# Block order and operand addresses of the token mixers, order of the first gates, the second norm and the joint w2 steps in a decoder trunk

## The chip, the core and the metric

The kernel runs on one core of a Trainium2 chip. The metric is the device time of one execution, in microseconds (us). The core's engines work side by side: TensorE (PE in the profile: matmuls, and PEld for the load of the stationary operand), VectorE (DVE), ScalarE (ACT), GpSimd (POOL) and SyncE (SP, which issues DMAs here). Each runs its own instructions in a fixed order and waits on semaphores of the others. Data moves between HBM and the on-chip memory by DMAs, issued from SP (mostly weights) and POOL (mostly spills and their reloads).

## The reference

One block of a decoder trunk on 512 tokens and 16 meta tokens, width 2048, in float32:

```python
u = rmsnorm(h, norm1_g[l])
proj = u @ w_in[l]
v_pool, v_lru, v_gelu, g_pool, g_lru = jnp.split(proj, IN_SPLITS, axis=-1)
pool_out = pool_mixer(v_pool, pool_w[l], pool_scale[l])
xc = causal_depthwise_conv(v_lru, conv_w[l], conv_b[l])
lru_out = rg_lru(xc, ...) * jax.nn.gelu(v_gelu)
merged = jax.nn.sigmoid(g_pool) * pool_out + jax.nn.sigmoid(g_lru) * lru_out
h = h + merged @ w_out[l]
u2 = rmsnorm(h, norm2_g[l])
h = h + jnp.square(jax.nn.relu(u2 @ mlp_w1[l])) @ mlp_w2[l]
out = rmsnorm(h, final_g)
```

`pool_mixer` subtracts each token from its mean over 2, 4, 8 or 16 positions (one width per 512 channels) and multiplies each group by a 512x512 matrix. `rg_lru` has two sigmoid gates per head of 256 channels (8 heads) and a linear recurrence over the positions. Of `w_in` the five parts of 2048 columns are called VP, VL, GE, GP and GL below (pool input, recurrence input, GELU input, two gates).

## The kernel before

Every float32 matrix product is made of three matmuls on a reduced float32 type (fp32r): each operand is the sum of a high and a low part, and `mm3` issues hi x hi, hi x lo and lo x hi into one accumulator. Weights come in tiles of 128x1024 from HBM (tile `raw` or `w`, SP). ACT copies the high part (`whi`, L137), DVE subtracts it for the low one (`wlo`, L138). A class `Weights` keeps the list of loads and splits: `W.next()` hands out the next split weight, `W.advance()` and `W.ready(n)` split ahead, `W.hold` and `W.behind` can tie a split or a sum behind another instruction.

**Mixers (0 to 477 us).** A table of jobs sets their order (the string `jobs`): V2 and VR project two output tiles each while the first norm is still made, VL_c and VP_c one tile of 128 channels each (16 input tiles, each 3 matmuls, over 528 tokens in blocks of 272 and 256 columns), GA_h the recurrence's gates of head h, PW_g the pool matrix of group g, F_k forms operands of the later gate projections and spills them (`fsp`). The activations lie in one tile `a1`; `ux(k, part)` gives the two blocks of input tile k. `products` runs over the two blocks of tokens, inside them over the input tiles that it is given; `in_proj` gives it one input tile at a time for VL and two at a time for VP. A VL tile is evacuated by DVE (`v`, L479) and goes through the convolution; a VP tile by DVE (`pv`, L558), then POOL adds the shifted copies (`pw`, L564), DVE makes the difference (`pd`, L567), and both parts of it go to `dsp_at(c)`, from where PW reads. The last job, PW_3, evacuates its tiles 12 to 15 by ACT (`po`, L586) into four buffers and stores them by DMA (`pl<-po`). The last head's recurrence (`lru`: ACT exp, tanh and Sqrt, DVE products and a scan) runs at the same time.

**Strassen steps.** The gate projections (GL, GE, GP for c = 0 to 7, 477 to 944 us) and the MLP's first matrix (32 steps, 1119 to 1734 us) take seven products of 2x2 blocks instead of eight, in the order x11, t1, t2, x21, t3, x22, t4, on three accumulators A, B and C. t1, t2, t3 and x22's weights are sums or differences, made on DVE (`sum`, `w`, L128). Between the products accumulators are copied by ACT: A after x11 (`p1`), B after t1 (`q5`), A after t2 (`u2`); `put` makes the four output blocks "11", "22", "12", "21". In the very first step (`gl0`) p1 and u2 lie in the tile `scale`. One of the seven input tiles of the gates' operands, k = 7 of x22, is shifted by some columns in its tile.

**Output projection and second norm.** From 945 to 1119 us w_out is multiplied and added to x. Then `middle()` in the first MLP step lets PE sum the squares over the partitions (`ps_r`, L993), from which `rho` follows in five steps on ACT and DVE.

**The second MLP matrix (1734 to 2348 us).** Again Strassen steps, with output tiles of 512 tokens x 256 channels. A few steps are joint (`strassen_pair`, groups [1,3], [2,4] and three at the end): two outputs share one weight, so that everything is done for two accumulators. Of p1, u2 and q5 there the second copy lies in a spare place: p1 and u2 in `scale`, q5 in the last quarter of the second output's tile `e`. The finished tile `e` is added into HBM by an accumulating DMA from POOL (`hsp<-e`, L1115, 512 KB), for groups up to step 31.

The order on each engine comes from a scheduler that keeps the program's order per engine where buffers and dependencies allow; buffers come from pools with a fixed number, and `issue_after` or a manual dependency ties single instructions.

## Time and profile before

| | us |
|---|---|
| median of the runs | 2389.03 (2384.92 to 2390.3, three runs) |
| profiled execution | 2389.73 |
| its span, first to last instruction | 2388.0 |
| first matmul starts | 6.3 |
| DVE busy, ACT busy | 1922.5, 1212.3 |
| mean granted TensorE clock | 0.994 |

A row of the page's list of groups has the line, engine, operation, tiles, shapes and count, then busy time, mean ns of one, and the idle time before it. A row of the waits has the engine and its instruction, the one that released it, and total, times and longest. A row of a timeline has start, duration, engine, line, operation, tiles, shapes and count (neighbours of one kind are merged), and in brackets the idle time before it with what ended it. A row of windows has the stretch, its length, and busy time and count of each engine, then the granted clock, the share of the DMA engines' time and GB/s. Matmuls overlap in their pipeline, so that their pace is read from counts and starts, not from the duration of one.

### The profile page before, as it was taken

The page shows a single profiled execution, that of the slowest core. Times are in us where ns is not written, and L with a number is a line of the kernel's source. Part 1 is how long each engine was busy: PE and PEld are TensorE (multiplying, and loading weights), DVE is VectorE, ACT ScalarE, POOL GpSimd, SP SyncE. Part 2 cuts the span into 40 slices and gives each one's busy share as a digit, 9 for nine tenths or more (in the row PEclk, how much of TensorE's full clock was granted, in tenths as well). Part 3 has the DMA queues.
Part 4 walks back from the last instruction along what each step waited for, and adds up shares of the span by engine and source line. Part 5 has one row for each costly group of instructions (what it writes and reads, how often), then busy time and mean ns, then how long its engine had stood idle before and what let it go on. Part 6 is the DMA issues. An engine that isn't in the chain of part 4 may idle for free. (4 is left out here: it accounts for less than half of the span.)

```text
span 2388.0 us, 46263 instructions
## 1 busy us (share of the span) xinstructions
PE 2347.3 (98%) x19254; PEld 2300.1 (96%) x19254; DVE 1922.5 (81%) x2356; ACT 1212.3 (51%) x1632; POOL 315.5 (13%) x435
## 2 busy tenths in 40 slices
PE   8999999999999999999999999999989999999997
PEld 8999999989999999888999999999989999999997
DVE  7866766588888887378989888888879888888877
ACT  6654645355555554244445444444455555555544
POOL 0224342300000001033000000000110000000013
PEclk9999999999999999999999999999999999999999
DMA  5255554654444447568544544555576666666662
GB/s 198 89 168 173 172 177 166 257 186 150 143 149 143 151 149 261 181 209 283 186 156 153 161 153 159 167 166 162 173 213 173 186 181 182 196 188 188 175 185 107
DMA packets 115858, 418.73 MB, mean 175 GB/s; under 512 B 14112, under 2 KB 18080, under 8 KB 113984
## 3 DMA queue, kind: packets, MB, share of 16 engines
q1 hardware_dynamic: 77040, 253.40, 32.9%
q0 software_dynamic: 38464, 162.29, 21.0%
q8 instruction: 150, 2.46, 0.4%
q14 instruction: 60, 0.49, 0.1%
q10 hardware_dynamic: 144, 0.10, 0.0%
HBM read 324.89 MB, written 90.31 MB: 174 GB/s over the span
## 5 line engine op out<-in xcount | busy, mean ns | idle before, releaser
L138 DVE TENSOR_TENSOR wlo<-raw,whi 128x1024 fp32r<-128x1024 f32 (+2 forms) x388 | 467.2, 1206 | 116.9 <-ACT whi L137 112.9
L137 ACT ACTIVATE whi<-raw 128x1024 fp32r<-128x1024 f32 (+2 forms) x388 | 398.9, 1034 | 318.0 <-issue 78.9
L137 ACT ACTIVATE whi<-sum 128x1024 fp32r<-128x1024 f32 (+3 forms) x267 | 279.0, 1045 | 454.2 <-DVE sum L128 234.8
L138 DVE TENSOR_TENSOR wlo<-sum,whi 128x1024 fp32r<-128x1024 f32 (+3 forms) x267 | 320.1, 1199 | 73.0 <-ACT whi L137 68.1
L370 PE MATMUL ps_A<-a,whi 128*128 128x256 f32 x2048 | 354.5, 277 | 0.0
L370 PE MATMUL ps_Ab<-a,whi 128*128 128x256 f32 x1728 | 308.8, 279 | 4.1 <-ACT u_b L746 2.1
L370 PEld LDWEIGHTS ps_A<-a,whi 128*128 128x128 f32 x2048 | 308.6, 188 | 0.7 <-issue 0.5
L370 PE MATMUL ps_A<-a,wlo 128*128 128x256 f32 x1024 | 282.9, 276 | 0.0
L370 PEld LDWEIGHTS ps_Ab<-a,whi 128*128 128x128 f32 x1728 | 263.9, 190 | 4.7 <-DVE a L1045 2.4
L370 PE MATMUL ps_Ab<-a,wlo 128*128 128x256 f32 x864 | 240.6, 279 | 0.0
L128 DVE TENSOR_TENSOR sum<-sum,raw 128x1024 f32<-128x1024 f32 (+4 forms) x178 | 213.7, 1201 | 5.5
L370 PEld LDWEIGHTS ps_A<-a,wlo 128*128 128x128 f32 x1024 | 192.3, 188 | 0.0
L370 PE MATMUL ps_B<-a,whi 128*128 128x256 f32 x1024 | 177.5, 276 | 0.0
L370 PEld LDWEIGHTS ps_Ab<-a,wlo 128*128 128x128 f32 x864 | 164.2, 190 | 0.0
L370 PE MATMUL ps_vl<-a,whi 128*128 128x272 f32 (+1 forms) x896 | 163.3, 285 | 0.0
L370 PE MATMUL ps_vp<-a,whi 128*128 128x256 f32 (+1 forms) x896 | 162.8, 284 | 0.0
L370 PE MATMUL ps_wo<-a,whi 128*128 128x512 f32 x512 | 158.0, 390 | 0.0
L370 PEld LDWEIGHTS ps_B<-a,whi 128*128 128x128 f32 x1024 | 154.2, 188 | 0.0
L370 PE MATMUL ps_Bb<-a,whi 128*128 128x256 f32 x864 | 152.5, 276 | 0.4 <-DVE a L1045 0.4
L370 PE MATMUL ps_B<-a,wlo 128*128 128x256 f32 x512 | 141.5, 276 | 0.0
L128 DVE TENSOR_TENSOR sum<-w,raw 128x1024 f32<-128x1024 f32 (+3 forms) x89 | 106.5, 1197 | 40.1 <-DMA raw<-w 39.7
L370 PEld LDWEIGHTS ps_vl<-a,whi 128*128 128x128 f32 x896 | 138.2, 189 | 0.3
(336 smaller groups left out, 5854.2 us busy)
## 6 DMA issues: line engine op xcount, KB each, us to landing
raw<-w SPq DMA_DIRECT2D x168, 512.0 KB, 4.3
raw<-w_in SPq DMA_DIRECT2D x135, 512.0 KB, 3.8
w<-w SPq DMA_DIRECT2D x56, 512.0 KB, 4.2
a<-ysp POOLq DMA_DIRECT2D x20, 896.0 KB, 6.1
hsp<-e POOLq DMA_DIRECT2D x33, 512.0 KB, 6.5
ysp<-t POOLq DMA_DIRECT2D x31, 512.0 KB, 4.9
w<-w_in SPq DMA_DIRECT2D x24, 512.0 KB, 3.9
ysp<-y POOLq DMA_DIRECT2D x31, 384.0 KB, 5.1
```

What stands on the lines that cost most here:

```text
L128: nc.vector.tensor_tensor(self.raw[o], self.raw[x], self.raw[y], op=ALU.add)
L137: nc.scalar.activation(hi[:, s], raw[:, s], AF.Copy)
L138: nc.vector.tensor_tensor(lo[:, s], raw[:, s], hi[:, s].bitcast(F32), op=ALU.subtract)
L370: PE.matmul(o, a, b, start=first and i == 0, stop=last and i == 2, skip_group_check=True)
```

## The change

It has five parts. (1) In the mixers `ux` gives other offsets: the blocks of 272 columns lie at 0 (input tiles 0 to 7) or 128 (8 to 15) modulo 256 bytes, those of 256 columns stay at 192, and k % 8 = 7 is shifted by 8 columns (32 bytes) from the others. VL and VP go through half of the input tiles for one block of tokens (8 x 3 = 24 matmuls), then for the other, with tile 7 first. The pool operands move from 192 to 0. (2) In the table of jobs F_3 stands behind VL_8 and PW_1, and the shifted sums of VP_15 are made by DVE. (3) The first gates: po14 and po15 go to a buffer of the pool of sums, both roots stand behind the p1 copy, the split first_set + 5 behind the u2 copy, and only sums from split first_set + 6 on stand behind the last scan. (4) The second norm: `ps_r` is issued behind t3, its values reuse the tiles ssq and v2, and the scaling of block "22" follows later. (5) The joint steps: q5's spare copy lies in `scale` (the place of p1), so "11" is put ahead of that copy; in the first two groups each e is added into HBM in three parts as they are finished (512 KB become 256, 128 and 128); the order of halves in e, h and the output changes to match.

```diff
@@ class Weights
+        self.roots, self.u2 = [], None
@@ the operands' places
     def ux(k, part):
         at = (2 * k + part) * XW
-        return a1[:, at : at + B0], a1[:, at + XW - HS : at + XW]
+        n, m = at + (16, 48)[k // 8], at + XW - HS
+        if k % 8 == 7:
+            n, m = at + (8, 40)[k // 8], m - 8
+        return a1[:, n : n + B0], a1[:, m : m + HS]
     def dsp_at(c):
-        at = 16 * HS + 2 * (c % 4) * SEQ
+        at = 16 * HS + 16 + 2 * (c % 4) * SEQ
...
-    jobs += " VP_7 GA_3 F_3 VL_8 PW_1 VL_9 F_4 VP_8 GA_4 VP_9 VL_10 F_5 VP_10 VL_11 F_6 VP_11 GA_5 VL_12 PW_2 F_7"
+    jobs += " VP_7 GA_3 VL_8 PW_1 F_3 VL_9 F_4 VP_8 GA_4 VP_9 VL_10 F_5 VP_10 VL_11 F_6 VP_11 GA_5 VL_12 PW_2 F_7"
@@ products, in_proj, job_VL, job_VP
-                    for k in ks:
+                    for i, k in enumerate(ks):
                         s = slice(k % 8 * P, (k % 8 + 1) * P)
-                        mm3(o, (hi[:, s], lo[:, s]), ux(k, 0)[b], ux(k, 1)[b], k == 0, k == KD - 1)
+                        mm3(o, (hi[:, s], lo[:, s]), ux(k, 0)[b], ux(k, 1)[b],
+                            k < 8 and i == 0 and (k == 0 or len(ks) == 8),
+                            k >= 8 and i == len(ks) - 1 and (k == KD - 1 or len(ks) == 8))
...
-                step = 1 if n > 1 else side
-                for k in range(8 * h, 8 * h + 8, step):
-                    for i in range(step):
+                if n == 1:
+                    products(ts, ws, [8 * h + k for k in order])
+                else:
+                    for k in range(8 * h, 8 * h + 8):
                         if head is not None:
-                            head(k + i)
-                    products(ts, ws, range(k, k + step))
+                            head(k)
+                        products(ts, ws, [k])
...
-            t, = in_proj(f"ps_vl{c}_", 1, side=1)
+            t, = in_proj(f"ps_vl{c}_", 1, order=(7, 0, 1, 2, 3, 4, 5, 6))
...
-            t, = in_proj(f"ps_vp{c}_", 1)
+            t, = in_proj(f"ps_vp{c}_", 1, order=(7, 0, 1, 2, 3, 4, 5, 6))
...
-                G.tensor_tensor(n[:, lo:T], s[:, lo:T], s[:, lo - win : T - win], op=ALU.add)
+                (V if c == KD - 1 else G).tensor_tensor(n[:, lo:T], s[:, lo:T], s[:, lo - win : T - win], op=ALU.add)
@@ the last head, the last pool group, the first gates
                 W.hold = lambda i: (tc.issue_after(opened.ins) if i == W.first_set
+                                    else tc.issue_after(W.u2.ins) if i == W.first_set + 5
                                     else contextlib.nullcontext())
...
-                if hd == HEADS - 1 and co == 0:
-                    W.root = root
+                if hd == HEADS - 1:
+                    W.roots.append(root)
...
-                W.behind = lambda i: (tc.issue_after(scan.ins) if 1 < i - W.first_set < 21
+                W.behind = lambda i: (tc.issue_after(scan.ins) if 5 < i - W.first_set < 21
...
-                z = (keep if g == 3 else tmp)(f"po{c}")[:, :SEQ]
+                if c == 14:
+                    last_two = sums_pool.tile([P, SW], F32, tag="sum", name="po14", bufs=2)
+                if c < 14:
+                    z = (keep if g == 3 else tmp)(f"po{c}")[:, :SEQ]
+                else:
+                    z = last_two[:, m % 2 * SEQ : (m % 2 + 1) * SEQ]
...
-                    tc.add_manual_dep(W.root.ins, done.ins.name,
...
+                    for root in W.roots:
+                        tc.add_manual_dep(root.ins, done.ins.name,
...
-        copied = S.activation(u2, A, AF.Copy)
+        copied = W.u2 = S.activation(u2, A, AF.Copy)
@@ strassen_pair
-        spare = {"p1": scale[:, :HS], "u2": scale[:, HS:SEQ], "q5": es[1][:, 3 * HS :]}
+        spare = {"p1": scale[:, :HS], "u2": scale[:, HS:SEQ], "q5": scale[:, :HS]}
...
+        put("11", C, p1)
         copy(q5[1:], B[1:])
-        put("11", C, p1)
@@ put_plain
-            n = a + 2 * b if by_half else 2 * a + b
+            n = 1 - a + 2 * b if by_half else 2 * a + b
@@ the second norm
+    def norm2(done):
+        t = bank("r", "", SEQ)
+        with tc.issue_after(done.ins):
+            PE.matmul(t, ones, ssq, start=True, stop=True, skip_group_check=True)
+        a, b = ssq, v2
...
+        norm_stage.close()
+        scaled_later.pop()()
...
+            if (j, c) == (0, "22") and z is not None:
+                scaled_later.append(lambda: put(c, o, None))
+                return
@@ the w2 steps
+    def adding(e, p):
+        put = put_plain(e, True)
+
+        def put_and_add(c, x, z):
+            put(c, x, z)
+            at = {"22": slice(HS, 3 * HS), "12": slice(3 * HS, 4 * HS), "21": slice(0, HS)}.get(c)
+            if at:
+                nc.gpsimd.dma_start(h_sp[p][:, at], e[:, at], accum_op=ALU.add)
+        return put_and_add
...
-        if t < JS + 2:
+        if n >= 2 and t < JS + 2:
             for x, e in zip(g, es):
                 nc.gpsimd.dma_start(h_sp[x % WIN], e, accum_op=ALU.add)
```

On PE, in the second half of a VP tile (`ps_vp`, a psum tile of one output tile; `a` the activations), the blocks of 272 and 256 columns alternated every two input tiles; before:

```order
L370 MATMUL ps_vp_0_1852<-a_84,wlo_1805 128x272
L370 MATMUL ps_vp_0_1852<-a_84,whi_1804 128x256 x2
L370 MATMUL ps_vp_0_1852<-a_84,wlo_1805 128x256
L370 MATMUL ps_vp_0_1852<-a_84,whi_1804 128x256 x2
L370 MATMUL ps_vp_0_1852<-a_84,wlo_1805 128x256
L370 MATMUL ps_vp_0_1852<-a_84,whi_1804 128x272 x2
```

and now, where eight pairs of rows with 272 columns stand ahead of eight with 256:

```order
L374 MATMUL ps_vp_0_1852<-a_84,whi_1804 128x272 x2
L374 MATMUL ps_vp_0_1852<-a_84,wlo_1805 128x272
L374 MATMUL ps_vp_0_1852<-a_84,whi_1804 128x256 x2
L374 MATMUL ps_vp_0_1852<-a_84,wlo_1805 128x256
L374 MATMUL ps_vp_0_1852<-a_84,whi_1804 128x256 x2
```

So the change of block comes once in 24 matmuls instead of once in six (in VL: once in three before).

On ACT, at the end of the mixers (po13 to po15, the last head's rows e and gs) and in the first gate step (p1 and u2 are the two rows `scale<-ps_Agl`); before:

```order
L586 ACTIVATE po14_5475<-ps_pw14_5462,par_71 128x512
L527 ACTIVATE e71_5507<-e71_5507 128x528
L137 ACTIVATE whi83_5499<-raw83_5424 128x1024
L586 ACTIVATE po15_5491<-ps_pw15_5478,par_71 128x512
L534 ACT_TABLE_LOAD
L534 ACTIVATE gs701_5374<-gs701_5374 128x528
L672 ACTIVATE scale_80<-ps_Agl0_5548 128x256
L534 ACTIVATE gs700_5359<-gs700_5359 128x528
L137 ACTIVATE whi84_5628<-w2181_5414 128x1024
L137 ACTIVATE whi85_5660<-sum80_5418 128x1024
L700 ACTIVATE scale_80<-ps_Agl0_5548 128x256
```

and now:

```order
L600 ACTIVATE po14_5475<-ps_pw15_5478,par_71 128x512
L138 ACTIVATE whi83_5498<-raw83_5424 128x1024
L536 ACTIVATE e71_5506<-e71_5506 128x528
L138 ACTIVATE whi84_5627<-w2181_5414 128x1024
L687 ACTIVATE scale_80<-ps_Agl0_5547 128x256
L543 ACT_TABLE_LOAD
L543 ACTIVATE gs700_5359<-gs700_5359 128x528
L543 ACTIVATE gs701_5374<-gs701_5374 128x528
L716 ACTIVATE scale_80<-ps_Agl0_5547 128x256
L138 ACTIVATE whi85_5659<-sum80_5418 128x1024
```

The table load and the roots moved behind the p1 copy, whi84 ahead of it, and whi85 behind the u2 copy.

On ACT, in the second joint step (outputs 2 and 4); before:

```order
L137 ACTIVATE whi519_20118<-w21345_19799 128x768
L746 ACTIVATE e4_20035<-ps_Bb4_20039 128x256
L746 ACTIVATE u2_b2_20043<-ps_Ab2_20036 128x256
L746 ACTIVATE scale_80<-ps_Ab4_20037 128x256
L1044 ACTIVATE a2_899<-a2_899 128x1536
```

and now:

```order
L138 ACTIVATE whi519_20119<-w21345_19796 128x768
L763 ACTIVATE u2_b2_20044<-ps_Ab2_20037 128x256
L763 ACTIVATE scale_80<-ps_Ab4_20038 128x256
L1068 ACTIVATE a2_899<-a2_899 128x1536
L1068 ACTIVATE a2_899<-a2_899 128x256
L138 ACTIVATE whi520_20147<-sum344_20028 128x768
L138 ACTIVATE whi521_20175<-raw346_19942 128x768
L138 ACTIVATE whi522_20205<-raw348_19988 128x640
L138 ACTIVATE whi523_20233<-sum348_20231 128x640
L763 ACTIVATE scale_80<-ps_Bb4_20040 128x256
```

The copy of B's second output, `e4<-ps_Bb4` before, stood ahead of the two u2 copies; now it is `scale<-ps_Bb4`, seven rows behind the second of them.

More of the change, by code (lines that the diff above doesn't have):

```diff
@@ L369, in mm3 @@
         for i, (a, b) in enumerate(((wh, mh), (wh, ml), (wl, mh))):
-            PE.matmul(o, a, b, start=first and i == 0, stop=last and i == 2, skip_group_check=True)
+            done = PE.matmul(o, a, b, start=first and i == 0, stop=last and i == 2, skip_group_check=True)
+        return done
     with ExitStack() as mx:
@@ L642, in build, with strassen @@
     ep = late.enter_context(tc.tile_pool(name="ep", bufs=1, side="right", reuse_waits="tile"))
-    def strassen(name, operand, put, between=None, head=None, middle=None, hooks={}):
+    def strassen(name, operand, put, between=None, head=None, middle=None, norm=None, hooks={}):
         A, B, C = (bank(x, name) for x in "ABC")
@@ L663, in tiles @@
                 s = slice(k * P, (k + 1) * P)
[L664 removed]
+                done = mm3(o, (w[0][:, s], w[1][:, s]), *xs[k], first and k == 0, k == len(xs) - 1)
+            return done
         def product(o, r, first):
             xs = operand(r)
[L668 removed]
+            return tiles(o, W.next(), xs, range(len(xs)), first)
         def after(r):
@@ L716, in strassen @@
         product(B, "x22", False)
+        if norm is not None:
+            norm(done)
         put("12", B, u2)
@@ L986, in build @@
     rho = scale[:, :SEQ]
+    scaled_later = []
     yp = y = None
@@ L1077, in build @@
             load_slot(0, nc.gpsimd)
-        strassen(j, X.get, put, **{0: dict(head=head, middle=middle), 8: dict(between=lambda: split_slot(0)), 31: dict(hooks=last)}.get(j, {}))
+        strassen(j, X.get, put, **{0: dict(head=head, middle=middle, norm=norm2), 8: dict(between=lambda: split_slot(0)), 31: dict(hooks=last)}.get(j, {}))
         S.activation(y, y, AF.Square)
```

59 lines of the change are left out of this document (27 added, 32 removed).

## The prediction

> **What bounds the kernel now.** I read the page first, for the share of each engine, then the waits of PE, then windows with the granted clock, then the timelines at the places where PE waits.
>
> ```profile
> PE 2347.3 (98%) x19254; PEld 2300.1 (96%) x19254; DVE 1922.5 (81%) x2356; ACT 1212.3 (51%) x1632; POOL 315.5 (13%) x435
> DVE  7866766588888887378989888888879888888877
> PE ps_Ab L370 <- ACT u_b L746: 5.3, 2, 3.3
> PE ps_Ab L370 <- DVE e L783: 2.8, 1, 2.8
> PE ps_Agl L370 <- ACT scale L700: 2.5, 1, 2.5
> PE ps_r L993 <- DVE ssq L859: 1.8, 1, 1.8
> PE ps_Bgl L370 <- ACT po L586: 1.5, 1, 1.5
> PE ps_Agl L370 <- ACT scale L672: 1.3, 1, 1.3
> PE ps_pw L365 <- DVE v L479: 1.3, 1, 1.3
> PE ps_pw L365 <- ACT a L570: 0.6, 1, 0.6
> PE ps_pw L365 <- DVE a L571: 0.2, 1, 0.2
> ```
>
> (The second row is DVE's busy share in 40 slices of 59.7 us, in tenths.) TensorE sets the end: it is busy for 2347.3 of 2388.0 us. So the change can gain in two ways: by the waits above (16.3 us, columns: total, times, longest), and by the pace of the matmuls themselves, which the busy share hides. The pace is a count per window (PE busy, count, PEld, ..., granted clock, DMA share, GB/s):
>
> ```profile
> 260.00:360.00 100.00, 100.00 (x829) 100.00 (x828) 1.00 0.51 169
> 700.00:760.00 60.00, 60.00 (x531) 60.00 (x530) 52.96 (x53) 32.27 (x42) 2.14 (x4) 1.00 0.45 150
> 493.80:500.62 6.82, 6.26 (x27) 0.50 0.91 328
> 1760.14:1766.97 6.83, 6.05 (x28) 6.05 (x29) 5.25 (x8) 5.44 (x9) 0.00 (x0) 0.50 0.04 15
> 2309.68:2313.10 3.42, 3.42 (x18) 3.42 (x18) 2.77 (x4) 1.83 (x3) 0.54 (x2) 0.50 1.00 375
> ```
>
> In the gate projections 60 us hold 530 whole matmuls of 256 columns: 113.2 ns each. In the mixers 100 us hold 828, half of 272 columns and half of 256: 120.8 ns, where 113.2 and 113.2 x 272/256 = 120.3 would give 116.7. So the mixers run 4.1 ns per matmul below a pace that the same shapes allow. The last three rows: after a wait of PE the granted clock is 0.50, for 6.8 or 3.4 us. A full-pace window of 6.82 us holds 60 matmuls; the first of them holds 27, which cost 3.06 us at pace, and 0.56 us of it is idle: the clock takes 3.2 us. The second takes 2.9 us so, the third (18 matmuls, 2.04 us) 1.4 us. The Trainium skill, page "TensorE: Matmul & The Clock Gate", section "Why this matters for your kernels", asks to avoid idle gaps of PE over about 3 us; here gaps of 2.5 and 2.05 us were already followed by the 0.50 clock, so the rows decide. By the page those two would cost only themselves, and the sum below would be 4.6 us smaller.
>
> **The change, part by part.**
>
> *Mixer inputs.* Why are they slow? The operands' offsets modulo 256 bytes, worked out from the tiles' sizes, are 192 for every block of the mixers before. The best evidence that this matters is a place where one loop runs at both paces:
>
> ```profile
> 914.00:926.00 12.00, 12.00 (x108) 12.00 (x107) 1.00 0.31 102
> 930.00:942.00 12.00, 12.00 (x103) 11.82 (x102) 1.00 1.05 404
> L370 PE MATMUL ps_vl<-a,whi 128*128 128x272 f32 (+1 forms) x896 | 163.3, 285 | 0.0
> L370 PE MATMUL ps_vp<-a,whi 128*128 128x256 f32 (+1 forms) x896 | 162.8, 284 | 0.0
> ```
>
> Same shape, clock 1.00 in both: 107 whole matmuls in 12 us (112.1 ns) against 102 (117.6 ns), after PE had stalled. In the trace the slow pace ends at 942.1, with the first operand tile read at another offset (the tiles shifted by 56 columns). So a slow state, once entered, seems to last until a tile at another offset is read. The change gives the mixers just that: the shifted tile comes first in each block of 24 matmuls (8 input tiles x 3 products), the blocks of 272 columns lie at 0 or 128. I take 3 of 24 matmuls at the old 120.8 and 21 at 116.7: mean 117.2, a saving of 3.6 ns. ps_vl and ps_vp have 896 matmuls with whi and half as many with wlo: 2 x 1344 = 2688 matmuls, 28 tiles of output. **2688 x 3.6 = -9.6 us.** If only the 256 blocks respond it is half, -4.8; if none, 0. V2 and VR (384 matmuls, order unchanged, offsets changed): between 0 and 384 x 4.1 = -1.6; I take -0.5.
>
> *Pooled operands* go from 192 to 0, the offset at which the output projection reads:
>
> ```profile
> 469.06 0.63 PE L365 MATMUL ps_pw<-a,whi 128*128 128x512 f32 x2
> 476.76 0.63 PE L365 MATMUL ps_pw<-a,whi 128*128 128x512 f32 x2
> 999.92 0.61 PE L370 MATMUL ps_wo<-a,whi 128*128 128x512 f32 x2
> 1005.36 0.61 PE L370 MATMUL ps_wo<-a,whi 128*128 128x512 f32 x2
> ```
>
> Between the first two rows lie 11 products of three: 7.70/33 = 233.3 ns; between the others 8: 5.44/24 = 226.7 ns, for the same 512 columns. 192 matmuls x 6.6 = **-1.3** (0 to -1.3).
>
> *F_3 behind VL_8 and PW_1.* Its splits (L613) stood on DVE ahead of the evacuation v (L479) that PE waited for; the 1.3 us wait of ps_pw goes. DVE's next work there is that evacuation itself; if F_3's splits then delay something later, DVE is only 70% busy in that slice (the fifth) and can make it up. **-1.3** (0 to -1.3).
>
> *VP_15's window sums on DVE.* Before, POOL does them with issues of a<-fsp between:
>
> ```profile
> 459.26 0.71 DVE L558 TENSOR_TENSOR pv<-ps_vp,scale 128x528 f32<-128x528 f32 x1 [2.38 <-PE ps_vp L370]
> 465.02 1.30 POOL L564 TENSOR_TENSOR pw<-pw 128x513 f32<-128x513 f32 x1
> 466.36 0.69 DVE L567 SCALAR_TENSOR_TENSOR pd<-pw,pv 128x512 f32<-128x512 f32 x1 [6.39 <-POOL pw L564]
> ```
>
> Four sums at DVE's 0.71 put pd at about 459.97 + 2.84 = 462.8, 3.5 us earlier, and DVE was idle for 6.4 us. The waits 0.6 + 0.2 go: **-0.8**. The four fills that stood between the sums are issued some 2 to 4 us earlier; nothing waits for them before 477.
>
> *First gates.* PE lost 1.5 + 1.3 + 2.5 in waits here and 3.2 to the clock. The rows that made them late:
>
> ```profile
> 481.09 0.69 ACT L586 ACTIVATE po<-ps_pw,par 128x512 f32<-128x512 f32 x1 [2.34 <-DMA pl<-po]
> 483.86 1.28 ACT L534 ACT_TABLE_LOAD   x1
> 485.70 0.36 ACT L672 ACTIVATE scale<-ps_Agl 128x256 f32<-128x256 f32 x1
> 490.75 1.07 ACT L137 ACTIVATE whi<-w 128x1024 fp32r<-128x1024 f32 x1 [4.16 <-DVE w L128]
> 492.73 1.25 DVE L545 TENSOR_TENSOR_SCAN xc<-n,gs 128x528 f32<-128x528 f32 x1
> 493.88 0.37 ACT L700 ACTIVATE scale<-ps_Agl 128x256 f32<-128x256 f32 x1
> ```
>
> po waited 2.34 us for a buffer that a DMA was still reading, and held the split behind it: now the last two po have a tile of their own. The table load and one root stood ahead of the p1 copy (485.70): both roots now come behind it. The u2 copy (493.88) stood behind whi<-w and whi<-sum, whose sums were late on DVE: now the split whi<-sum is behind u2, and only sums from the seventh split on wait for the scan. What is late next is DVE: two scans (1.25 each), the recurrence's other rows (about 0.7 each) and splits of 1.2 each, in the 14 us of seven products. Laid out row by row with these durations it keeps up: the weight parts of the sixth product (x22) are ready at about 488.4 and PE needs them at 489.3, those of the seventh at 489.5 against 492, on the clock of the rows above. I take all of it, with 0.4 for the slow pace after the stalls: 5.3 + 3.2 + 0.4 = **-8.9**; if DVE is some 2 us late at one product, a wait and half a clock stretch come back, -5; with both at two products 0.
>
> *Norm 2.* ps_r moves behind t3, so the 1.8 us wait goes. But DVE is what PE meets next:
>
> ```profile
> 1133.04 1.22 DVE L138 TENSOR_TENSOR wlo<-sum,whi 128x1024 fp32r<-128x1024 f32 x1
> ```
>
> This split, which x22 needs, ends at 1134.3 behind unbroken DVE work, most of which stays. PE would reach it 1.8 us earlier and wait. **-0.3**; all of it gone would be -1.8, one more DVE row (0.7) ahead of it +0.7.
>
> *Joint w2 steps.* Before, q5 of the second output lies in the e tile, which an accumulating DMA still reads:
>
> ```profile
> 1749.19 1.79 POOL L1115 DMA_DIRECT2D hsp<-e  x2 [6.77 <-ACT e L781]
> 1760.21 0.38 ACT L746 ACTIVATE e<-ps_Bb 128x256 f32<-128x256 f32 x1 [5.92 <-DMA hsp<-e]
> 1760.38 0.83 DVE L128 TENSOR_TENSOR sum<-w,raw 128x640 f32<-128x640 f32 x1 [3.51 <-DMA raw<-w]
> 2308.69 0.38 ACT L746 ACTIVATE e<-ps_Bb 128x256 f32<-128x256 f32 x1 [5.74 <-DMA hsp<-e]
> q0 software_dynamic: 1241, 5.54, 40.5%
> q1 hardware_dynamic: 2061, 4.89, 26.8%
> ```
>
> (The last two: packets, MB, share of 16 DMA engines, from 1736 to 1790.) ACT then holds the u2 copies behind this e, and PE waits for them. With q5 in scale the copy e goes from there. At 2309: the wait of 2.05, the clock's 1.4 and about 0.3 of slow pace, **-3.7**. At 1760 the wait of 3.3 goes too, but DVE's sum waits for its own load until 1760.38, and the split made of it is needed by x22; PE then stops about 2 us later and starts again at about 1764 instead of making up ground until 1765.8: -1.5. In the first joint step q5's copy now stands behind the put of "11": +0.7. The accumulation by quarters starts some 4 us earlier, so that its transfers should end earlier and the wait of 2.8 for e (L783) may go or stay. q0's packets take 0.405 x 16 x 54 us / 1241 = 282 ns for 4.5 KB, q1's 112 ns for 2.4 KB, so time goes with bytes, and smaller quarters should not cost much more. First two steps together: **-2.5**, from -7 (the last wait and its clock gone) to +3 (the stall comes back elsewhere with its clock).
>
> **Sum**: 9.6 + 0.5 + 1.3 + 1.3 + 0.8 + 8.9 + 0.3 + 3.7 + 2.5 = 28.9 us less. The profiled execution took 2389.73 (span 2388.0 and 1.7 around it), 0.7 above the median of 2389.03. 2389.7 - 28.9 = **2361 us**.
>
> **The rivals.**
> 1. *Offsets do nothing.* The mixers' pace could come from the column count or from DMA traffic, and 942 could be chance. For it: 930 to 942 also has a DMA share of 1.05; against: the mixers are slow at 0.51, the gates fast at 0.45. Then 9.6 + 0.5 + 1.3 are missing: 2372. The Trainium skill, same page, section "Back-to-back issue gap", gives the gap by column count alone (N/2.4 + 2.5 ns), without an offset; by it the change leaves the mixers as they are. Its formula makes 109 ns of 256 columns, where the trace has 113.2 and 117.6.
> 2. *The first gates get a new wait.* DVE is late at a product, PE stalls and the clock falls: -9 becomes -3 to 0, 2367 to 2370. For it: DVE's rows leave less than 1 us of slack there.
> 3. *Accumulation by quarters clogs the DMA queues.* Three transfers take the place of one. Four e of 128 packets of 282 ns over 16 engines take 9.0 us; if a packet costs that whatever its size, twelve transfers take 27 us, 18 us more, in a stretch where loads already arrive late. PE would stall for 9 us in each step with 6.8 us at half clock (3.4 lost) behind: 2 x 12.4 = +25, the 2.5 are lost, and one later step meets late loads as well, with a wait like the present 3.3 and 2.9 of clock: +6. 2361 + 33.5 = 2395, slower than before. It decides where a 1 KB packet costs over about 270 ns; q1's 112 ns speaks against it.
>
> **How the numbers follow.** Forecast (2354 to 2366, with partial pace gains) 0.55; rival 1 (2372, with a gain in the gates) 0.19; rival 2 0.17; rival 3, 0.06, of which 0.03 within 0.2% of before and 0.03 beyond; more gained than all this 0.03. 0.2% is 4.8 us, about what a measurement of this kernel can tell. Low end: 2361 with joint steps at -7, V2 and VR at -1.6 and norm 2 at -1.8, 2361 - 7.1, and 2 for my rounding of paces: **2352**. High end: rival 1 with half of rival 2: **2376**. Faster 0.93, within 0.2% 0.04, slower 0.03.
>
> **What would show it.** Mixers: 100 us windows with about 854 matmuls instead of 829; still 829 proves rival 1. Pooled: 33 matmuls in 7.5 us. First gates: no wait of ps_Agl or ps_Bgl and no 0.50 clock near 490. Joint steps: ACT without a wait for hsp<-e, and the u2 copies right behind their products; DMA queue q0 with more packets of shorter time. Norm 2: PE waits for wlo near 1132 instead of for ssq. The prediction is wrong if the mixers' pace stays, or if new 0.50 stretches stand where none were.

## The result and the profile after

The changed kernel takes 2372.13 us (median of 4 runs, 2370.74 to 2373.0), the kernel before 2387.19 (median of 4 runs): a ratio of 0.9935 [0.9918, 0.9953]. That is inside the predicted range and 11 us above its centre. The profiled executions, 2372.0 (span 2370.2) against 2389.73 (span 2388.0), differ by 17.7 us, the medians by 15.1: the profiled execution of the kernel before lies near the upper end of its runs (2384.92 to 2390.3).

From the page of the changed kernel, the row of busy times, and below it the waits of PE (columns: total, times, longest, us):

```profile
PE 2341.4 (99%) x19254; PEld 2296.0 (97%) x19254; DVE 1924.4 (81%) x2360; ACT 1213.4 (51%) x1632; POOL 318.5 (13%) x439
```

```profile
PE ps_v L374 <- ACT whi L138: 6.6, 1, 6.6
PE ps_Ab L374 <- ACT p_b L763: 1.9, 1, 1.9
PE ps_Ab L374 <- DVE a L1069: 1.8, 1, 1.8
...
PE ps_Ab L374 <- DVE e L800: 1.0, 1, 1.0
PE ps_B L374 <- DVE wlo L139: 1.0, 1, 1.0
...
PE ps_A L374 <- ACT p L687: 0.6, 1, 0.6
...
PE ps_Age L374 <- ACT p_ge L687: 0.3, 1, 0.3
PE ga L374 <- DVE xs L499: 0.2, 1, 0.2
```

All the waits that the prediction listed are gone except the one for e (L783, now L800; 2.8 before, 1.0 now). New are `ACT p_b` with 1.9 and, in the place of `DVE ssq` with 1.8, `ACT p` (at 1120.7) and `DVE wlo` (at 1125.0) with 1.6 together. Since PE is busy for 99% of the span, what else was gained or lost lies in the pace of its matmuls. Windows of the changed kernel, the first in the mixers, the second in the gate projections (columns as in the prediction):

```profile
260.00:360.00 100.00, 99.77 (x820) 99.55 (x820) 1.00 0.54 174
700.00:760.00 60.00, 60.00 (x531) 60.00 (x531) 52.52 (x53) 31.83 (x40) 2.15 (x4) 1.00 0.44 147
```

The gates keep their pace (531 as before), but the mixers hold **820** matmuls in 100 us, fewer than the 829 before and far from the 854 of the forecast. (0.2 us of the window is idle, which is 2 matmuls.)

The starts of the same matmuls in both profiled executions divide the difference into stages:

| stage | predicted, us | measured, us |
|---|---|---|
| start to PW_3 (mixers, three pool groups) | -12.4 | +0.9 |
| PW_3 | -1.1 | -1.6 |
| first gate step | -8.9 | -8.3 |
| rest of gates, w_out | 0 | +0.6 |
| MLP steps 0 and 1 with the second norm | -0.3 | +0.2 |
| MLP steps 2 to 31 | 0 | -0.3 |
| joint steps 1/3 and 2/4 and steps 5 to 7 | -2.5 | -7.2 |
| joint steps from 33 | -3.7 | -2.0 |
| sum | -28.9 | -17.7 |

The first row is made up of the start (+0.3), the wait of ps_pw for v (-1.3), a new wait of ga for xs (+0.2), three pool groups (48 matmuls each at -6.6 ns, -0.95) and the rest, **+2.7 from the mixers' matmuls**, where -10.1 was forecast (9.6 and 0.5). Of these 2.7, VL and VP hold 2.1: added up from the start of each matmul to the start of the next, they take 324.9 us before and 327.0 now. The mean of a matmul of 272 columns went from 124.9 to 125.8 ns in VL and from 123.6 to 126.1 in VP, that of 256 columns from 117.2 to 117.0 in VL, and it stayed at 117.7 in VP. The blocks of 256 columns are not all alike now: 8 of the 56 run at 114.3 ns, the other 48 at 117.7 to 117.9. The remaining 0.6 lies in V2, VR and the gates and is mostly scatter, since V2 takes 25.7 to 27.0 us in executions that have the same code for it.

The ACT rows of the changed kernel in the first gate step (start, duration, us) answer to those of the prediction:

```profile
476.96 0.69 ACT L600 ACTIVATE po<-ps_pw,par 128x512 f32<-128x512 f32 x1
480.63 0.36 ACT L687 ACTIVATE scale<-ps_Agl 128x256 f32<-128x256 f32 x1
481.01 1.28 ACT L543 ACT_TABLE_LOAD   x1
485.44 0.39 ACT L716 ACTIVATE scale<-ps_Agl 128x256 f32<-128x256 f32 x1 [1.95 <-PE ps_Agl L374]
```

po no longer waits for a DMA, the table load follows the p1 copy, and the u2 copy waits for PE itself. The step takes 20.01 us instead of 28.32.

### The profile page after: what moved, and what is told of

Read it like the earlier page. It is cut to its first block, busy times and chain, and to the rows that moved or that the text cites. A ratio compares the mean times of both kernels' runs of the same rounds, so it can differ in the third digit from the quotient of the medians.

```text
span 2370.2 us, 46286 instructions
## 1 busy us (share of the span) xinstructions
PE 2341.4 (99%) x19254; PEld 2296.0 (97%) x19254; DVE 1924.4 (81%) x2360; ACT 1213.4 (51%) x1632; POOL 318.5 (13%) x439
## 4 chain that ended last, share of the span: by engine, by line
PE 67%; issue 23%; DVE 4%; POOL 2%; DMA 2%; ACT 1%; POOLq 0%; DVEq 0%; ACTq 0%; SPq 0%
PE ps_Ab L374 13%; PE ps_wo L374 7%; PE ps_Bb L374 6%; PE ps_vp L374 5%; PE ps_vl L374 5%; PE ps_Agp L374 4%; PE ps_Age L374 4%; PE ps_Agl L374 3%; PE ps_Cb L374 3%; PE ps_Bgp L374 2%; PE ps_A L374 2%; PE ps_Bge L374 2%; PE ps_Bgl L374 2%; PE ga L374 1%; PE ps_pw L369 1%
## 5 line engine op out<-in xcount | busy, mean ns | idle before, releaser
L139 DVE TENSOR_TENSOR wlo<-raw,whi 128x1024 fp32r<-128x1024 f32 (+2 forms) x388 | 466.7, 1204 | 119.4 <-ACT whi L138 115.1
L138 ACT ACTIVATE whi<-sum 128x1024 fp32r<-128x1024 f32 (+3 forms) x267 | 278.9, 1045 | 448.3 <-DVE sum L129 236.6
L374 PE MATMUL ps_vp<-a,whi 128*128 128x272 f32 (+1 forms) x896 | 164.4, 285 | 0.0
L374 PEld LDWEIGHTS ps_vp<-a,whi 128*128 128x128 f32 x896 | 139.3, 189 | 0.1
```

What stands on the lines that cost most here:

```text
L138: nc.scalar.activation(hi[:, s], raw[:, s], AF.Copy)
L139: nc.vector.tensor_tensor(lo[:, s], raw[:, s], hi[:, s].bitcast(F32), op=ALU.subtract)
L374: done = PE.matmul(o, a, b, start=first and i == 0, stop=last and i == 2, skip_group_check=True)
```

## The experiments

Each of the ten variants below is the changed kernel with one part altered (three parts in the last); two more kernels measure matmuls alone. Each group shares its runs of the kernel before, so the ratios to that are what is compared (the changed kernel: 0.9935).

**The mixers: old code, old offsets, old order.** The first takes all mixer edits back (offsets, order of blocks, tile 7 first):

```diff
-        n, m = at + (16, 48)[k // 8], at + XW - HS
-        if k % 8 == 7:
-            n, m = at + (8, 40)[k // 8], m - 8
-        return a1[:, n : n + B0], a1[:, m : m + HS]
+        return a1[:, at : at + B0], a1[:, at + XW - HS : at + XW]
...
-            t, = in_proj(f"ps_vl{c}_", 1, order=(7, 0, 1, 2, 3, 4, 5, 6))
+            t, = in_proj(f"ps_vl{c}_", 1, side=1)
...
-            t, = in_proj(f"ps_vp{c}_", 1, order=(7, 0, 1, 2, 3, 4, 5, 6))
+            t, = in_proj(f"ps_vp{c}_", 1)
```

> The changed kernel with the mixer inputs as before (offsets 192, blocks alternating, no tile leading); all else of the change stays. In the changed kernel PW_3 starts at 465.9 us, 0.9 later than before, although the pooled operands and F_3 gained 2.2 on the way. Theory 1, the new blocks and offsets themselves cost about 3 us: PW_3 starts at about 463 and the time falls by about 3 us, to 2369. Rival, something else in the mixers slowed them (the moved F_3, DMAs): PW_3 stays at about 466 and the time at 2372.

The second takes back only the offsets in `ux` (the first five lines), the third only the order (the rest).

> The changed kernel with only the operand offsets of the mixer inputs as before (all 192, no shifted tile), blocks of 24 kept. If the offsets 0 and 128 make the blocks of 272 slower: the mean of a 272-column matmul falls from 125.9 to about 124 ns and PW_3 starts near 463. If the order in blocks of 24 costs it: PW_3 stays near 466. If the leading shifted tile is what lets some blocks of 256 run at 113 ns (one first half in four does so now): these go back to 118 and PW_3 comes later than 466.

> The changed kernel with only the order of the mixer inputs as before (272 and 256 alternating), new offsets kept. If the offsets cost: 272-column matmuls stay at about 126 ns and PW_3 starts near 466 or later. If the order costs: they fall to 124 and PW_3 starts near 463.

Measured: old mixers 2372.42 us, 0.9933 [0.9919, 0.9947]; old offsets 2371.14, 0.9934 [0.9917, 0.995]; old order 2374.28, 0.9947 [0.9933, 0.9961]. None of the three ratios can be told from the changed kernel's, so no gain of its mixer edits shows in the total. The profiles tell more than the totals. Where PW_3 starts (groups by tile; columns: count, shortest/median/longest ns, first and last start in us), before, changed, and with the old offsets:

```profile
L365 PE MATMUL ps_pw<-a,whi x26: 393/394/497, 464.9 to 474.9; 128*128 128x512 f32 x26
```

```profile
L369 PE MATMUL ps_pw<-a,whi x28: 389/389/395, 465.9 to 474.9; 128*128 128x512 f32 x28
```

```profile
L366 PE MATMUL ps_pw<-a,whi x32: 388/389/389, 463.1 to 473.5; 128*128 128x512 f32 x32
```

With the old order it starts at 466.36, with old mixers at 464.91, between the two times expected of that variant (463 and 466). These starts alone decide little: in the five variants below that keep the changed mixers, PW_3 starts anywhere from 464.2 to 468.1. The time that VL and VP take, added up as above, is steady, 326.9 to 327.0 us in the changed kernel and in those five. It is 324.9 before and with old mixers, 324.2 with the old offsets and 327.5 with the old order. So the new offsets cost 2.6 us in the old order and 2.8 in the new one, and the order itself gains 0.7 at the old offsets and about 0.5 at the new. PW_3 does not follow in full, since a quicker pace is partly lost again: with old mixers ga waits 1.4 us for xs instead of 0.2. That offsets do nothing is refuted: they act, the wrong way.

**Matmuls alone at each offset.** A kernel of its own runs series of 96 matmuls (48 for 512 columns), 32 or 16 operand pairs x 3 products, of one width and offset, then mixed series:

```python
CASES = [(f"x{q}", [(256, o)] * 32) for q, o in zip("abcdefgh", range(0, 256, 32))]
CASES += [(f"y{q}", [(272, o)] * 32) for q, o in zip("abcdefgh", range(0, 256, 32))]
CASES += [(f"z{q}", [(512, o)] * 16) for q, o in zip("aceg", range(0, 256, 64))]
...
```

> A kernel of its own that computes nothing of the reference: it runs series of 48 to 96 matmuls like the mixers' (high and low parts, eight input tiles in turn) on idle engines, each series of one width (256, 272, 512 columns) at one operand offset modulo 256 bytes, then the mixers' mixed orders; before each series TensorE waits for ACT. Theory of the prediction (the offset decides): 256 columns at 113 ns at some offsets and 118 at others, 512 at 226.7 at 0 and 233 at 192, 272 at 120.4 at 0 and about 124 at 192. Rival 1, the width decides: 272 at 124 to 126 at every offset. Rival 2, traffic of the other engines decides: all series at 113.3, 120.4 and 226.7.

Windows of 10 us: 256 columns at 0, 64, 160 and 192, then 272 at 0, 64, 128, 160 and 192, then 512 at 0 and 192:

```profile
24.50:34.50 10.00, 10.00 (x86) 1.00 0.01 2
48.50:58.50 10.00, 10.00 (x88) 1.00 0.01 2
84.50:94.50 10.00, 10.00 (x87) 1.00 0.01 2
96.50:106.50 10.00, 10.00 (x90) 1.00 0.01 2
120.50:130.50 10.00, 10.00 (x81) 1.00 0.01 2
145.50:155.50 10.00, 10.00 (x80) 1.00 0.01 2
171.50:181.50 10.00, 10.00 (x81) 1.00 0.01 2
184.50:194.50 10.00, 10.00 (x84) 1.00 0.01 2
197.00:207.00 10.00, 10.00 (x83) 1.00 0.01 2
222.00:232.00 10.00, 10.00 (x46) 1.00 0.01 2
257.00:267.00 10.00, 10.00 (x45) 1.00 0.00 0
```

The means from start to start, in ns:

| offset modulo 256 | 0 | 32 | 64 | 96 | 128 | 160 | 192 | 224 |
|---|---|---|---|---|---|---|---|---|
| 256 columns | 120.0 | 117.8 | 117.8 | 120.0 | 118.7 | 118.7 | **113.3** | 118.3 |
| 272 columns | 126.7 | 125.9 | 126.7 | 125.3 | 126.7 | **123.3** | **123.3** | 125.3 |
| 512 columns | **226.7** | | 228.9 | | 232.7 | | 233.3 | |

The pace depends on width and offset together, with no DMA running (share 0.01). The pooled operands' 0 is the best for 512 columns, but 0 and 128 are the worst for 272, and none of the eight offsets reaches the assumed 120.3. Besides, 256 columns at 192 have two paces: 113.3 when alone, 117.8 for all 93 matmuls behind three at 160 that open a series, and 117.7 behind 272 columns at 192. Three at 160 in the middle of a quick series leave it quick (113.3 behind them), so what decides is not the tile ahead alone. The change's own pattern gave 125.5/117.7/126.2/117.9 for its four blocks: its tile ahead did not bring the 256 blocks to the quick pace.

**What brings it.** A second such kernel runs the mixers' pattern (blocks of 24: 272, 256, 272, 256 columns) with other offsets and lead tiles, and other widths.

> A kernel of its own that computes nothing of the reference, like m1_pace: first blocks of 24 matmuls of 272 and 24 of 256 columns in turn (272 at offset 192 or 160, 256 at 192, with or without one leading tile at another offset), then series of 264, 240 and 288 columns at each offset. In m1_pace 272 columns took 123.3 ns at best (160 and 192) and 256 columns 113.3 at 192 after a wait, 117.8 after blocks of 272. If a leading tile at the right offset brings the 256 blocks to 113.3, some rows of the first kinds show it. If not, all show 117.8 to 120. An even cut of 264 + 264 would need under 118.3 each to beat 236.6 for the pair.

Two of its passes of 96 matmuls (groups by tile): all blocks at 192, and the same with a first 256 tile at 160:

```profile
L214 PE MATMUL ps_pn<-a,whi x64: 281/283/393, 23.2 to 34.6; 128*128 128x272 f32 x32, 128*128 128x256 f32 x32
...
L214 PE MATMUL ps_pf<-a,whi x64: 276/284/394, 96.2 to 107.5; 128*128 128x272 f32 x32, 128*128 128x256 f32 x32
```

All at 192 the blocks run at 123.3/117.8/123.3/117.7 ns. With the lead tile of the 256 blocks at 160, or at 0 or 32, those run at 114.1 to 115.0; at 96 and 128 one of two blocks does (114.5 and 115.1); at 64 and 224 it does nothing. Shifting the lead tile of the 272 blocks does nothing (117.7). So the shifted tile works, if the blocks of 272 stay at 192. With the blocks of 272 at 160 none is needed: without a lead tile the 256 columns run at 113.6 ns and the 272 at 123.6; no variant of the kernel tried this. Other cuts of the 528 columns are no better: 264 + 264 need at least 240.0 ns a pair, 272 + 256 need 236.6.

**The changed kernel with its 272 columns at 192:**

```diff
-        n, m = at + (16, 48)[k // 8], at + XW - HS
-        if k % 8 == 7:
-            n, m = at + (8, 40)[k // 8], m - 8
-        return a1[:, n : n + B0], a1[:, m : m + HS]
+        m = at + XW - HS - (8 if k % 8 == 7 else 0)
+        return a1[:, at : at + B0], a1[:, m : m + HS]
```

> The changed kernel with only the 272-column blocks back at 192 (none shifted); the 256 blocks stay at 192 with the leading tile at 160, order in blocks of 24 stays. On idle engines (m1_pace, m2_widths) a pass of 96 matmuls took 11.20 us in the changed kernel's pattern, 11.08 with all at 192, 10.93 in this one: 272 columns 123.4 ns instead of 125.5 and 126.2, 256 columns 114.1 to 114.8 instead of 117.8. If that holds beside the other engines' work: 28 tiles x 0.27 = 7.6 us, PW_3 starts at about 458.3 instead of 465.9, time about 2364.5. Rival, the state that makes 256 columns fast does not hold in the kernel (DMA and other engines, the gates' matmuls between): only the 272 blocks gain, 28 x 48 x 2.5 ns = 3.4 us, PW_3 at 462.5 to 463 as in e2_old_offsets, time 2369.

Measured: 2368.53 us, 0.9923 [0.9906, 0.9939]. The interval still overlaps the changed kernel's; the profile is clearer: 50 us of mixer matmuls, 290 to 340, in the changed kernel and in this one, and where this one's PW_3 starts:

```profile
290.00:340.00 50.00, 50.00 (x412) 50.00 (x412) 1.00 0.53 164
```

```profile
290.00:340.00 50.00, 50.00 (x424) 50.00 (x423) 1.00 0.56 181
```

```profile
L367 PE MATMUL ps_pw<-a,whi x32: 388/389/389, 459.9 to 470.3; 128*128 128x512 f32 x32
```

The pace gains what was expected: VL and VP take 319.4 us, 7.6 less than in the changed kernel, and all 56 blocks of 256 columns run at 114.1 to 114.8 ns. PW_3 starts only 6.0 us earlier, since ga takes 3.1 longer: it waits 1.3 for DVE's xs and 0.8 for ACT's (0.2 and 0 in the changed kernel), where the quicker PE arrives too soon. (The start, V2 and VR are 1.4 us quicker in this execution, most of it scatter of V2.)

**The first gates as before** (po14 and po15 in a tile of their own, roots, and split rules undone):

```diff
-                                    else tc.issue_after(W.u2.ins) if i == W.first_set + 5
...
-                if hd == HEADS - 1:
+                if hd == HEADS - 1 and co == 0:
...
-                W.behind = lambda i: (tc.issue_after(scan.ins) if 5 < i - W.first_set < 21
+                W.behind = lambda i: (tc.issue_after(scan.ins) if 1 < i - W.first_set < 21
...
-                if c == 14:
-                    last_two = sums_pool.tile([P, SW], F32, tag="sum", name="po14", bufs=2)
...
+                z = (keep if g == 3 else tmp)(f"po{c}")[:, :SEQ]
```

> The changed kernel with the first gates' part undone: po14 and po15 in the old buffers, only one root behind p1, no hold on the split first_set + 5, sums from the third split on behind the scan. Prediction's theory: the waits of ps_Bgl and ps_Agl and a stretch of 0.50 clock come back, first matmul of gl to first of ge takes about 28.3 us instead of 20.0, time +8. Rival, the gain came from the earlier end of VP_15's sums (which stay on DVE here): about 20 to 22 us, time +0 to +2.

Measured: 2380.16 us, 0.9972 [0.9961, 0.9982], the only variant whose interval lies wholly above the changed kernel's. The gate step takes 27.37 us instead of 20.01 (20.0 to 20.1 in all nine variants that keep this part). ACT's rows of this variant, and its window behind PE's wait:

```profile
480.70 0.69 ACT L594 ACTIVATE po<-ps_pw,par 128x512 f32<-128x512 f32 x1 [4.11 <-DMA pl<-po]
484.62 0.69 ACT L594 ACTIVATE po<-ps_pw,par 128x512 f32<-128x512 f32 x1 [1.30 <-DMA pl<-po]
488.71 0.37 ACT L681 ACTIVATE scale<-ps_Agl 128x256 f32<-128x256 f32 x1
```

```profile
489.20:492.60 3.40, 3.40 (x16) 3.40 (x17) 3.29 (x7) 0.41 (x1) 0.00 (x0) 0.51 0.35 134
```

Both po wait for the DMA that still reads their buffer, the p1 copy comes 8 us later (2.2 of it because the whole execution runs later by then), PE stalls for 4.3 us and runs its next 3.4 us at a clock of 0.51. This is the chain that the prediction described. (In this variant the u2 copy still stands ahead of the split behind it, so that piece was not tried alone.)

**The joint steps.** Three variants: q5's spare copy back in the e tile (and "11" put behind it), the accumulation whole instead of in parts, and two splits of the last output's y moved behind the u2 copies of the step [34, 36].

```diff
-        spare = {"p1": scale[:, :HS], "u2": scale[:, HS:SEQ], "q5": scale[:, :HS]}
+        spare = {"p1": scale[:, :HS], "u2": scale[:, HS:SEQ], "q5": es[1][:, 3 * HS :]}
```

> The changed kernel with only q5's spare copy back in the e tile (and the put of 11 behind it). Theory of the prediction: ACT's copy e waits for the accumulating DMA again, PE for u2: at the second joint step a wait of 1 to 3 us, at step 33 one of 2.0 with or without a stretch of half clock; together +4 to +8 us over the changed kernel. Rival, the accumulation by quarters alone has ended its DMA in time: no wait at the second step, only the 2 us at step 33.

```diff
-            puts = [adding(e, x % WIN) if n < 2 else put_plain(e, True) for e, x in zip(es, g)]
+            puts = [put_plain(e, True) for e in es]
...
-        if n >= 2 and t < JS + 2:
+        if t < JS + 2:
```

> The changed kernel with only the accumulation of the first two joint steps in whole tiles of 512 KB again, when each step is done. If the quarters gain: first matmul of step 1 to first of step 8 takes more than the 78.07 us of the changed kernel, by 2 to 4 us, with a wait for e (L800) near 1770 of 2 to 3 us instead of 1.05. If they only cost DMA time: 78 us or less.

```diff
+            def between():
+                split_slot(n + 3)
+                while t == JS + 3 and last:
+                    last.pop()()
...
-        if t == JS + 3:
-            while last:
-                last.pop()()
```

> The changed kernel with one more edit: the two splits of the last y (a<-a, L1174) stand behind the u2 copies of the joint step [34,36] on ACT instead of ahead of its p1 copy. In the changed kernel ACT waits 7.92 us for their load (DMA a<-ysp) and PE then 1.90 for p_b. If that wait is what took half of the last joint steps' gain: the wait of p_b goes, the way from the start of step 33 to the end shortens by about 2 us, nothing new waits. Rival, another late thing (DVE's sums, splits of weights) stands right behind it: PE waits there instead and less than 0.5 us is gained.

Measured: spare in e 2378.75 us, 0.9957 [0.9941, 0.9973]; whole accumulation 2378.11, 0.9962 [0.9949, 0.9975]; late splits 2370.2, 0.9929 [0.9913, 0.9945]. The steps 1 to 7 take 78.07 us in the changed kernel, 80.92 with the spare in e (+2.9) and 81.25 with the whole accumulation (+3.2). In the eight variants that keep both edits they take 77.3 to 79.6, so both costs stand clear of the scatter, but their sizes are known to 1 or 2 us only; the intervals of the totals overlap the changed kernel's. ACT with the spare in e, then DVE with the whole accumulation, then DVE in the changed kernel:

```profile
1749.13 0.39 ACT L763 ACTIVATE e<-ps_Bb 128x256 f32<-128x256 f32 x1 [4.49 <-DMA hsp<-e]
2293.83 0.38 ACT L763 ACTIVATE e<-ps_Bb 128x256 f32<-128x256 f32 x1 [5.73 <-DMA hsp<-e]
```

```profile
1753.81 0.82 DVE L129 TENSOR_TENSOR sum<-w,raw 128x640 f32<-128x640 f32 x1 [3.43 <-DMA raw<-w]
```

```profile
1751.06 0.82 DVE L129 TENSOR_TENSOR sum<-w,raw 128x640 f32<-128x640 f32 x1 [1.20 <-DMA raw<-w]
```

Each edit removes its own wait. The one for raw is 3.4 and 3.5 us in the two kernels with whole tiles and at most 1.2 in the ten with parts, so the parts bring it down; that the load gets its turn sooner when the accumulating transfers start earlier is the likely reason, not shown. The wait for e, expected to grow to 2 or 3 us with whole tiles, did not occur: PE stops there for whi and for scale, 1.4 each, with 6.8 us at half clock. With the spare in e the two waits for u2 came as expected (4.0 together), but from step 33 on only 0.5 is lost, since p_b no longer waits there. A packet of the smaller parts costs less time: from 1736 to 1790 q0 moves 2088 packets in the changed kernel:

```profile
q0 software_dynamic: 2088, 3.77, 38.8%
```

0.388 x 16 x 54 us / 2088 = 160 ns for 1.8 KB, against 282 for 4.5 KB before, which ends rival 3.

At the end, with the steps from 33, a load had been late all along. In the changed kernel (ACT; then the POOL row that issues the load), and before:

```profile
2303.29 0.63 ACT L1174 ACTIVATE a<-a 128x512 fp32r<-128x512 f32 x1 [7.92 <-DMA a<-ysp]
...
2306.77 0.38 ACT L763 ACTIVATE p_b<-ps_Ab 128x256 f32<-128x256 f32 x1
```

```profile
2297.63 0.54 POOL L1170 DMA_DIRECT2D a<-ysp  x1 [3.90 <-PE ps_Ab L374]
```

```profile
2318.74 0.63 ACT L1137 ACTIVATE a<-a 128x512 fp32r<-128x512 f32 x1 [3.73 <-DMA a<-ysp]
```

Before, ACT waited 3.73 us there, and PE was late enough not to notice. Now ACT waits 7.92, holds the p_b copy behind it, and PE stops for 1.9. The variant with late splits shows that this accounts for the lost half: the wait is gone, and two steps from 33 take 38.18 us instead of 40.37. (The total cannot be told from the changed kernel's.)

**The second norm as before** (`ps_r` ahead of the tile y0, "22" scaled in its place):

```diff
...
+        t = bank("r", "", SEQ)
+        PE.matmul(t, ones, ssq, start=True, stop=True, skip_group_check=True)
+        V.scalar_tensor_tensor(rho, t, EPS * D, v2, op0=ALU.add, op1=ALU.mult)
...
-    def norm2(done):
...
-            if (j, c) == (0, "22") and z is not None:
-                scaled_later.append(lambda: put(c, o, None))
-                return
```

> The changed kernel with only the second norm as before (ps_r ahead of t3's splits in program order, its own tiles, 22 scaled at once). First matmul of MLP step 0 to first of step 2 took 41.80 us before, 41.95 in the changed kernel, and 43.9 to 44.3 in three of the experiments, where waits of PE for p and wlo near 1121 came with it. If the moved norm gains nothing: 41.8 here, time within 1 us of the changed kernel. If it gains its 1.8 us wait: 43.5 or more here. If it costs: always near 41.8 here and 2 us less than in the runs with 44.

Measured: 2375.09 us, 0.9947 [0.9932, 0.9962]. Inconclusive: MLP steps 0 and 1 take 40.83 us here, 41.80 before and 44.07 in the next variant, all with the old norm; with the new one they take 41.95 in the changed kernel and 41.3 to 44.7 in the eight variants that have it. No gain of the new norm shows. And the total here includes a stretch at half clock at 2307 that has nothing to do with the norm:

```profile
2307.00:2311.00 4.00, 3.76 (x18) 3.76 (x19) 4.00 (x5) 1.86 (x5) 0.00 (x0) 0.57 0.00 0
```

**Together**: the 272 columns at 192, the late splits and the old norm in one kernel.

> The changed kernel with three edits together: 272-column blocks at 192 (e8_272_at_192), the last splits behind the u2 copies (e5_late_splits), the second norm as before (e10_old_norm). If they add up: from the changed kernel's profile 6.0 us less in the mixers, 2.0 less at the last joint steps and 1 less at MLP step 0, span about 2361 and a median of 2362 to 2365. If the old norm costs its own wait of ps_r or the late splits are late once the stage in front runs earlier: only the 6 us, median 2366 to 2368, with a wait of ps_r near 1114 of over 0.9 or of p_b near 2300.

Measured: 2367.34 us, 0.9914 [0.99, 0.9927], the least of all (its interval still overlaps the changed kernel's), and in the range of the second case, 2366 to 2368. The waits of PE say why:

```profile
PE ps_r L1009 <- DVE ssq L874: 2.1, 1, 2.1
...
PE ga L372 <- ACT xs L496: 1.0, 1, 1.0
PE ga L372 <- DVE xs L497: 1.0, 1, 1.0
```

The old norm's wait is 2.1 us here, with a half clock behind it (0.50 from 1117.2 to 1120.6), so this version pays for the old norm; ga takes 4.0 us longer than in the changed kernel, 2.0 of it in waits and some in a half clock behind them (0.50 from 277.5 to 280.9). The late splits keep their gain: no wait of p_b is left.

## Why the prediction was right or wrong

The time lies in the predicted range, but the largest term failed, by the sign that the prediction had set for itself: the mixers' pace stayed. That the time lies in the range all the same is in part luck: the joint steps won 4.7 us more than forecast, and the range reached that far because of rival 1, whose reason is refuted.

- **Mixer inputs: wrong, and the whole miss** (-10.1 forecast with V2 and VR, +2.7 measured). The failing step is "113.2 x 272/256 = 120.3": it carried a pace from 256 columns at 192 over to 272 columns at 0 and 128, where the trace showed no such matmul. Measured, 272 columns take 126.7 ns there, and 123.3 at best. The second half of that step, that the slow pace lasts until a tile at another offset is read, is true only where the neighbouring blocks lie at 192; with them at 0 and 128, 48 of the 56 blocks of 256 stayed at 117.7 to 117.9; why eight ran at 114.3 is open.
- **Rival 1** gave 2372, the time that came, for another reason. "Offsets do nothing" is refuted by the variants: the offsets are worth 2.6 to 2.8 us against the change, and putting the 272 columns back alone makes VL and VP 7.6 shorter. The Trainium skill, page "TensorE: Matmul & The Clock Gate", section "Back-to-back issue gap", gives the isolated gap of a matmul by its column count, without an offset (109 ns for 256 columns); the runs disagree (113.3 to 120.0 ns for 256 columns, by offset).
- **Pooled operands, F_3, VP_15: right.** A matmul of 512 columns takes 226.7 ns, as forecast, and the waits of F_3 and VP_15 are gone; these three were not undone alone. A new wait of ga for xs (0.2) takes a little back.
- **First gates: right** (-8.9 forecast, -8.3 measured, +7.4 when undone). DVE kept up, and the granted clock is 1.00 from 476 to 497, so rival 2 did not occur; one wait of 0.3 is left at the step's end (`ACT p_ge`).
- **Norm 2: not settled** (-0.3, measured +0.2 for its steps). The mechanism was right: PE meets `ACT p` for 0.6 and `wlo` for 1.0 instead of ssq for 1.8. The size can't be told, since the steps vary by 3 us between executions.
- **First two joint steps: right in kind, too small** (-2.5, measured -7.2, just beyond its range of -7 to +3). The term counted a load of raw as fixed at 1760.38; with the parts of the accumulation it came sooner. Undone one at a time, the parts are worth 3.2 us and the spare copy 2.9.
- **Step 33: right place, half the gain** (-3.7, measured -2.0). Missing was the question what ACT is late with next: the load a<-ysp, 3.73 us late already in the trace of before.

The waits that the prediction lists add up to 17.3 us, not 16.3; its sum does not use that figure.

By terms: 12.8 lost in the mixers, 1.7 at step 33, 0.5 at norm 2 and 0.6 at the first gates; 4.7 won in the joint steps; the rest is 0.6 or less each.

## What to carry to other kernels

Before operands are moved to another address, measure the exact width at the exact offset, and in the order of the neighbours, in a small kernel: a pace seen with another shape does not carry over. When a wait is removed, look on the same queue for the next thing that is already late but hidden, since it becomes the new wait. An accumulating transfer that starts in parts as its pieces are finished can free loads that come behind it.

## What the runs showed of the hardware

- The pace of these fp32r matmuls depends on the byte offset of the moving operand modulo 256, by 6% at 256 columns (113.3 to 120.0 ns) and by 3% at 272 and 512, and the best offset differs by width. At one of them (256 columns at 192) there are two paces, 113.3 and 117.8, and what ran just before decides. What in the hardware does this stays open.
- A wait of about 2 us is followed by a clock near 0.50 in one execution and not in another. In the changed kernel a wait of 1.8 was, one of 1.9 was not:

```profile
1729.00:1733.00 4.00, 3.92 (x19) 3.38 (x20) 4.00 (x7) 2.76 (x6) 0.08 (x1) 0.64 0.94 384
2307.30:2310.70 3.40, 3.40 (x30) 3.40 (x31) 3.40 (x4) 1.35 (x3) 0.00 (x0) 1.00 0.00 0
```

  The place of the wait decides. The three stretches in the prediction's windows start at 493.80, 1760.14 and 2309.68 us, which is 371.0 and 161.0 times 3.413 us apart, and they last one or two such lengths: the clock changes on a fixed grid. Laid over the twelve kernel traces from the first full clock to 2350 us, PE was idle for 1.78 us or more in 19 windows of the grid, and the half clock followed each time; of 34 windows with 1.0 to 1.7 us idle it followed two. (The ends of matmuls are modelled, so these idle times are estimates.) The wait of 1.8 above fell into one window (1.86 idle with a short gap beside it), the one of 1.9 left 1.70 in its window. Before, the first of these two waits was divided between two windows (1.12 idle in each), and no half clock followed: the new one at 1730 comes from where the wait fell.

  The Trainium skill, same page, section "What's actually happening", has a window of about 3.4 us that runs freely; the traces agree with it. But that section asks for an idle window, and here about half a window was enough.

  Such a stretch costs 1.4 to 3.2 us by the prediction's windows, which may explain why the variants with more waits in the joint steps spread over 6 to 7 us between runs (spare in e 2373.33 to 2379.55); the kernel before spreads as much (2383.94 to 2391.2).
